# Retention and SSD layer on eight cores: state outputs in tile layout, keys scaled at evacuation, less work on GpSimd, new scheduling constants

## The chip, the cores and the metric

The kernel runs on one Trainium2 chip (trn2), the same program on all 8 cores, each with its own requests. The metric is the device time of the slowest core, in microseconds (us). Every run also gives the span of each core and its mean granted TensorE clock. Some executions of these kernels were in a second, slower state, in which some cores show a lower clock and the time is longer: cores 4 and 5 at 0.933 to 0.939, where the same kernel's fast runs had every core at 0.964 or more. Such runs are marked slow here, and comparisons use fast runs alone.

Names in the profile: PE is TensorE, PEld its weight load, DVE is VectorE, ACT ScalarE, POOL GpSimd, SP the sync engine that issues many of the transfers.

## The reference, cut

One layer of a hybrid backbone, shortened here (casts and some arguments are left out). Two groups of tokens share the weights: context (two sequences of 256 per core) and latent (one sequence of 1024 per core, scans starting from given states).

```python
def trunk_layer(x, mod, rope, s_ret0, s_ssd0, p):
    sh1, sc1, g1, sh2, sc2, g2 = jnp.split(mod, 6, axis=-1)
    h = x * (1 + sc1) + sh1
    proj = h @ p['w_in']
    q, k, v, g, z, xbc, dt_raw = jnp.split(proj, IN_SPLITS, axis=-1)
    ...                                   # retention: 4 heads, chunked two-way scan, gated RMS norm
    o_ret, sr_f, sr_b = bidir_scan(q, k, v, v, lg_f, lg_b, s_ret0[0], s_ret0[1])
    ...                                   # Mamba-2 SSD: 8 heads, conv, chunked two-way scan
    y, ss_f, ss_b = bidir_scan(cm, bm, xsf * dt_f[..., None], xsf * dt_b[..., None], la_f, la_b, ...)
    o_ssd = (rms_norm(y * silu(z)) * p['ssd_norm_w']).astype(x.dtype)
    mix = jnp.concatenate([o_ret, o_ssd], axis=-1) @ p['w_out']
    x = layer_norm(ALPHA * x + g1 * mix, p['ln1_g'], p['ln1_b'])
    h2 = x * (1 + sc2) + sh2
    ffn = (silu(h2 @ p['w_gate']) * (h2 @ p['w_up'])) @ p['w_down']
    x = layer_norm(ALPHA * x + g2 * ffn, p['ln2_g'], p['ln2_b'])
    return x, s_ret, s_ssd                # the context's final states are outputs too
```

Inside a scan the state of a chunk is the sum over its tokens of tail · kᵀv: the decay `tail` may be put on the keys or on the values.

## The kernel before

The kernel is a Python program that builds a graph of operations. A list scheduler then gives each operation an engine and a place in that engine's order, by a cost model of its own, and an allocator lays all buffers into one arena. So an edit to one operation can move everything else. Times that the scheduler believes are called *planned* below; they are not times of the chip. The parts that the argument touches:

```python
# constants of the scheduler: priorities, order of stages, ring depths, and LD: after which buffer's
# work a weight load is let go
LV = dict(ht=1.1, conv=0.5, ..., retA=1.3, retB=1, ..., evB=0.5, outA=1.6, outB=0.9, ...)
SEQ = ("ssdA", "headA", "ssdB", "ada", "headB", "outA", "outB")
LD = dict(..., wo0="a0", wo1="a3", ..., ln1="oB", g0="b2", g1="b0", ...)
# ... cut ...
    oret_d = do("oret", [2, 2, 4, 128, 128])          # context states, retention
    ossd_d = do("ossd", [2, 2, 8, 128, 64])           # context states, SSD
# ... cut ...
    def affine(out, in_, scale, bias, eng=(ACT, DVE)):
        ...
        if DVE in eng:
            alts[DVE] = (vcost(DVE, out, [in_], "ts") + 0.08,
                         lambda e: e.tensor_scalar(out=R(out), in0=R(in_), scalar1=R(scale), scalar2=R(bias), op0=ALU.mult, op1=ALU.add))
# ... cut ...  a weight slab loaded as f32 in halves, and cast on the core
    def half_load(name, dst, src, q, after=()):
        s = P.buf("%s_f%d" % (name, q), 2048)
        o = P.dma(SP, s, src[:, q * 2048:(q + 1) * 2048], after=after)
        for i in range(2):
            cp(dst[:, q * 2048 + i * 1024:q * 2048 + (i + 1) * 1024], s[:, i * 1024:(i + 1) * 1024], (ACT, DVE, POOL))
# ... cut ...  start: small biases of the convolution, and the scaled input hs1 (xT1 is the second latent half)
            affine(hs3[ck][:, kt, :], xT[(ck, q)][...], sc1p[q][:, kt % 4, c:c + 1], 0.0)
        ts(nb3[:, f, :], p3, -1.0, ALU.mult)
        tt(cb3[:, f, :], p3, wsum[:, f].unsqueeze(2).to_broadcast([128, 4, 2]), ALU.mult)
# ... cut ...  SSD block: small row copies feed a matmul's operand, on the SP queue
        for s_ in range(3):
            P.dma(SP, sx[96 + s_:97 + s_, :].rearrange("p (r n) -> p r n", r=16), rsT[g][32 * s_:32 * s_ + 16, tok])
# ... cut ...  retention head: values scaled by tail from SBUF or PSUM, keys transposed and copied
                tt(vs[...], vsrc[...], tailw4[:, d, h, :]..., ALU.mult, EN["vs"])
            cp(kt_[:, c_ * 512:c_ * 512 + 512], ps, (ACT, DVE))
            P.dma(SP, oret_d[:, :, h].rearrange("s d p e -> p s d e"), stS.rearrange("p (s d e) -> p s d e", s=2, d=2), is_out=True)
# ... cut ...  the parameters of the first layer norm, multiplied in on GpSimd, one token tile at a time
    late.append((P.dma(SP, ln1, brow(R_LN1G, 2048)), "ln1"))
            tt(x1[t], x1[t], ln1[:, 0:1024], ALU.mult, POOL)
            tt(x1[t], x1[t], ln1[:, 1024:2048], ALU.add, POOL)
```

Of the kernel before, what the change touches and what calls it, by code (L numbers as in the profile page):

```python
# [22 lines left out]
class Op:  # L23
    __slots__ = ("idx", "eng", "alts", "is_dma", "nbytes", "deps", "inc", "cval", "fin", "npend", "succ", "start", "key",
                 "allocs", "touch", "sem", "is_out", "table", "tag", "cost", "ready", "done", "fn", "w", "pal")

    def __init__(self, idx, alts, key, tag):
        self.idx, self.alts, self.key, self.tag = idx, alts, key, tag
        self.eng, self.fn, self.cost = None, None, 0.0
        self.is_dma, self.nbytes, self.deps, self.inc, self.cval = False, 0, set(), False, 0  # L30
        self.fin = self.start = 0.0
        self.npend, self.succ, self.allocs, self.touch = 0, [], [], []
        self.sem, self.is_out, self.table, self.ready, self.done = None, False, None, 0.0, False
        self.w, self.pal = [], []
# [90 lines left out]
class Prog:  # L125
# [17 lines left out]
    def add(self, alts, reads, writes, table=None, after=()):  # L143
# [33 lines left out]
        for a in after:  # L177
            if a is not None:
                o.deps.add(a)
        return o  # L180
# [30 lines left out]
    def schedule(self, extra):  # L211
# [85 lines left out]
        busy = {e: 0.0 for e in ENGS}  # L297
        while nd < n:
# [41 lines left out]
            st = max(t, o.ready)  # L340
            if o.allocs:
# [19 lines left out]
            o.eng, o.fn, o.cost, o.start, o.done = e, fn, cost, st, True  # L361
            tcur[e] = st + cost
# [27 lines left out]
    def place(self, slack):  # L390
        live = []
        for b in self.bufs:
            if not b.ops:
                b.off = 0
                continue
            t0 = min(min([o.start] + [a.start for a in o.pal]) for o in b.ops)
            t1 = max(o.fin for o in b.ops)
            live.append((t0, t1, b))
# [41 lines left out]
    def emit(self, stack):  # L440
# [61 lines left out]
        def make(engname):  # L502
# [32 lines left out]
LV = dict(ht=1.1, conv=0.5, tm=1.1, prep=1, ssdA=1, ssdB=1.1, ssdi=0, retA=1.3, retB=1, reti=0.02, headA=2, headB=1.7, evA=0, evB=0.5, outA=1.6,  # L535
          outB=0.9, evoA=0.7, evoB=0.7, ada=1.2)
OPT = dict(rope="")
ENG = dict(yn="V", vs="VP", wg="VP", y2="P", g="")
SEQ = ("ssdA", "headA", "ssdB", "ada", "headB", "outA", "outB")
RING = dict(W=3, P=2, y1=2, y2=2, yb=2, xw=3, Sd=3, Sf=3, Sfb=1, hB=3, hA=4, vs=1, kt=2, PT=1, sq=2, rg=1, qf=3, rp=2, xr=3)  # L540
LD = dict(w2="x1", h10="p1A", h11="p0B", a4="p0B", a5="p1A", h12="z11", a6="p1B", a8="z3", h13="z3", a7="b0", a9="a3", wo0="a0", wo1="a3", h00="a2",
          h01="a2", a10="a2", a11="b1", h02="oA", h03="b1", rope="z7", S0f="oA", xr1="b1", xr0="b1", gate01="a2", gate00="b3", ln1="oB", g0="b2", g1="b0",
          g2="oB", g3="b2", g4="oB", g5="f0", g6="f4", g7="f4", g8="f5", g9="f2", g10="f3", wd0="f4", wd1="f5", wd2="f9", wd3="f10", ln2="f10", gate11="f9",
# [5 lines left out]
C_CVEC, C_BADA, C_CONVW, C_CONVB, C_LN1G, C_LN1B, C_N = 0, 16, 64, 104, 112, 120, 128  # L549
# [33 lines left out]
def build():  # L583
# [19 lines left out]
    oret_d = do("oret", [2, 2, 4, 128, 128])  # L603
    ossd_d = do("ossd", [2, 2, 8, 128, 64])
# [49 lines left out]
    def vcost(eng, out, ins, kind):  # L654
# [5 lines left out]
        if any(inps(v) for v in ins):  # L660
            return 0.17 + n * 0.00103
        if kind in ("copy", "ts"):
            return 0.12 + n * 0.00075
# [34 lines left out]
    def affine(out, in_, scale, bias, eng=(ACT, DVE)):  # L698
# [3 lines left out]
        if DVE in eng:  # L702
# [48 lines left out]
    def half_load(name, dst, src, q, after=()):  # L751
# [3 lines left out]
        for i in range(2):  # L755
            cp(dst[:, q * 2048 + i * 1024:q * 2048 + (i + 1) * 1024], s[:, i * 1024:(i + 1) * 1024], (ACT, DVE, POOL))
# [42 lines left out]
    nwb = P.buf("nwb", 512)  # L799
    P.dma(SP, nwb, brow(R_NW, 512), after=[xl[7]])  # L800
# [85 lines left out]
    for ct in range(8):  # L886
        for j in range(5):
            ts(diagw4[:, ct, j, :], ident_f, cols[:, C_CONVW + ct * 5 + j:C_CONVW + ct * 5 + j + 1], ALU.mult, eng=(DVE, POOL))
    dI = P.buf("dI", 1024, BF16)
    dI3 = dI.rearrange("p (h m) -> p h m", h=8)  # L890
    for h in range(8):
        ts(dI3[:, h, :], ident_f, smalls[:, 32 + h:33 + h], ALU.mult, eng=(DVE, POOL))
# [282 lines left out]
    nws = P.buf("nws", 512)  # L1175
# [10 lines left out]
    def state_update(d, t, S, nxt):  # L1186
# [4 lines left out]
        tt(v8(xw), v8(xs_tm[t]), bc8(w), ALU.mult, POOL)  # L1191
# [7 lines left out]
        tt(v8(sd), v8(S), bc8(EXPO[g][:, q, 32 + d * 8:40 + d * 8]), ALU.mult, POOL)  # L1199
# [5 lines left out]
    def ssd_seq(g, t0, nb, s0):  # L1205
# [8 lines left out]
        for i in range(nb - 1, -1, -1):  # L1214
            if S is not None:
                Rb[i] = P.buf("R%d" % (t0 + i), 512, BF16)
                cp(Rb[i], S, (ACT, POOL))
# [4 lines left out]
        if not s0:  # L1222
            P.dma(SP, ossd_d[(t0 - 8) // 2, 1].rearrange("h n e -> n h e"), v8(S), is_out=True)
# [4 lines left out]
        for i in range(nb):  # L1228
# [3 lines left out]
            if S is not None:  # L1232
                Sb = rSfb()
                cp(Sb, S, (ACT, POOL))
# [6 lines left out]
        if not s0:  # L1241
            P.dma(SP, ossd_d[(t0 - 8) // 2, 0].rearrange("h n e -> n h e"), v8(S), is_out=True)
# [3 lines left out]
    def ssd_block(g, t, Sb, Rb):  # L1246
# [43 lines left out]
        tt(y1, cur, z_tm[t], ALU.mult, DVE if cur is y else POOL)  # L1290
# [4 lines left out]
        yn, yb = ry2(), ryb()  # L1295
        tt(yn, y1, nws, ALU.mult, EN["yn"])
        affine(yb, yn, sm[:, 1:2], 0.0, (ACT,))
# [4 lines left out]
        cp(oT[t // 4][:, :, o_:o_ + 128], ps.rearrange("p (j t) -> p j t", j=4), (ACT, DVE))  # L1302

    P.level = LV_BG
    ts(nws, nwb, math.sqrt(512.0), ALU.mult)
# [7 lines left out]
    rvs = {GA: Ring("vsA", RING["vs"], 1024, BF16), GB: Ring("vsB", RING["vs"], 1536, BF16)}  # L1313
    rkt = {GA: Ring("ktA", RING["kt"], 512, BF16), GB: Ring("ktB", RING["kt"], 1024, BF16)}
# [6 lines left out]
    def ret_unit(h, ck, b0, T, v3, cross):  # L1321
# [6 lines left out]
        for d in range(2):  # L1328
            if cross[0]:
                qf[d] = rqf()  # L1330
                tt(c2(qf[d]), c2(q), b2(rowt4[:, h, d, :]), ALU.mult, (DVE, POOL))
# [19 lines left out]
        tt(rg, rg, T["g"][:, b0:b0 + 512], ALU.mult, POOL)  # L1351
# [5 lines left out]
    def head(g, h, wload, lv):  # L1357
# [5 lines left out]
        for j, name in ((0, "q"), (1, "k"), (3, "g")):  # L1363
            for c_, ck in enumerate(CK[g]):
# [7 lines left out]
                else:  # L1372
# [10 lines left out]
                    tt(b, tA, tB, ALU.add, POOL)  # L1383
        vs = rvs[g]()
        voff = lambda d, j: (d * 4 + j) * 128
        for c_, ck in enumerate(CK[g]):
# [7 lines left out]
            for d in range(2):  # L1394
                a_, n_ = (0, 4) if g == GA or c_ == d else ((2, 2) if c_ == 0 else (0, 2))
                v0 = voff(d, c_ * 4 + a_)
                vsrc = T["v"][:, c_ * 512:c_ * 512 + 512] if "P" in ENG["vs"] else ps
                tt(vs[:, v0:v0 + n_ * 128].rearrange("p (c j e) -> p c j e", j=2, e=128), vsrc[:, a_ * 128:(a_ + n_) * 128].rearrange("p (c j e) -> p c j e", j=2, e=128),
                   tailw4[:, d, h, :].unsqueeze(1).unsqueeze(3).to_broadcast([128, n_ // 2, 2, 128]), ALU.mult, EN["vs"])
# [3 lines left out]
        kt_ = rkt[g]()  # L1403
        for c_ in range(len(CK[g])):
# [3 lines left out]
            cp(kt_[:, c_ * 512:c_ * 512 + 512], ps, (ACT, DVE))  # L1408
        k3 = kt_.rearrange("p (j e) -> p j e", e=128)
        v3 = T["v"].rearrange("p (j e) -> p j e", e=128)  # L1410
        vt = lambda d, j: vs[:, voff(d, j):voff(d, j) + 128]
        if g == GA:
            ps = P.ps("mix")
            for s_ in range(2):
                for d in range(2):
                    for j in range(2):
                        mm(ps[:, (s_ * 2 + d) * 128:(s_ * 2 + d) * 128 + 128], k3[:, s_ * 2 + j, :], vt(d, s_ * 2 + j), j == 0, j == 1)
            stS = rstS()
            cp(stS, ps, (ACT, DVE))
            P.dma(SP, oret_d[:, :, h].rearrange("s d p e -> p s d e"), stS.rearrange("p (s d e) -> p s d e", s=2, d=2), is_out=True)  # L1420
            ret_unit(h, 2, 0, T, v3, [[], []])
        else:
            pu = [P.ps("mix"), P.ps("mix", 256)]
            for s_ in range(3):
                for d in range(2):
                    c = 3 - s_ if d else s_
                    for j in range(2):
                        mm(pu[s_ // 2][:, (s_ % 2) * 256 + d * 128:(s_ % 2) * 256 + d * 128 + 128], k3[:, c * 2 + j, :], vt(d, c * 2 + j), j == 0, j == 1)
# [4 lines left out]
            for s_ in range(3):  # L1433
                t_, sb = rSt(), rSb()
                tt(de(t_), prev, gd, ALU.mult, (DVE, POOL))
                u = pu[s_ // 2][:, (s_ % 2) * 256:(s_ % 2) * 256 + 256]
                if s_ < 2:
                    sf = rSr()
                    tt(sf, t_, u, ALU.add)
                    cp(sb, sf, (ACT, POOL))  # L1440
# [159 lines left out]
    def stage(name):  # L1600
# [19 lines left out]
        elif name == "headB":  # L1620
# [3 lines left out]
            cp(S0b, S0f, (POOL,))  # L1624
# [37 lines left out]
def _prep_inputs(inp):  # L1662
# [39 lines left out]
    for i in range(8):  # L1702
# [7 lines left out]
        cols[:, C_LN1B:C_LN1B + 8] = f(inp["ln1_b"])[0].reshape(8, 128).T  # L1710
        m = dict(shared)
# [21 lines left out]
```

## Time and profile before

| | before |
|---|---|
| time, median of 4 runs | 766.73 us (763.62 to 767.23) |
| spans of the 8 cores in the profiled run | 742.1 to 762.4, mean 753.7 us |
| core 5 (slowest): PE / DVE / ACT / POOL busy | 88 / 55 / 39 / 44% |

First the table of busy time by stretch of time, for core 5. Each column of an engine is its busy time in that stretch, with the count of instructions; then come the granted clock, the share of the DMA engines and their rate. TensorE's idle time in a stretch is the stretch less its busy time.

```profile
core 5: us, PE busy (x) PEld busy (x) DVE busy (x) ACT busy (x) POOL busy (x), PEclk, DMA share, GB/s
0.00:80.00 80.00, 50.75 (x471) 28.44 (x471) 36.74 (x118) 37.11 (x69) 27.03 (x76) 0.91 0.92 228
80.00:200.00 120.00, 111.56 (x879) 63.03 (x880) 91.69 (x183) 91.00 (x145) 76.18 (x88) 0.97 0.53 102
200.00:240.00 40.00, 20.82 (x169) 12.48 (x166) 19.84 (x32) 18.10 (x31) 17.79 (x21) 0.74 0.85 155
240.00:360.00 120.00, 105.81 (x912) 63.47 (x913) 107.30 (x175) 61.76 (x101) 82.15 (x84) 1.00 0.49 106
...
400.00:430.00 30.00, 19.76 (x109) 12.27 (x108) 22.91 (x24) 12.87 (x19) 16.22 (x9) 0.83 0.47 106
430.00:740.00 310.00, 310.00 (x1438) 140.52 (x1437) 100.32 (x177) 56.05 (x92) 100.61 (x71) 1.00 0.28 61
```

Read it from the bottom. From 430 us on TensorE is busy all the time, so what happens there can only shift. All that can be won lies in the idle time before: 29.2 us at the start, 19.2 us in 200 to 240, 14.2 us in 240 to 360, 10.2 us in 400 to 430. Two of these are single waits. The timeline of core 5 near 216 us (start, duration, engine, operation; in brackets the idle time before it and what ended it):

```profile
215.96 0.22 PE L622 MATMUL psum<-arena 128*128 128x128 bf16 x1 [2.02 <-DVE arena L670]
232.06 2.18 PE L622 MATMUL psum<-arena 128*128 128x256 bf16 x8 [15.88 <-DVE arena L670]
...
208.81 4.50 POOL L670 TENSOR_TENSOR arena<-arena 128x512 bf16<-128x512 bf16 x4 [2.69 <-ACT arena L647]
227.54 0.59 POOL L185 DMA_DIRECT2D arena<-w_out  x1 [14.23 <-DMA oret<-arena]
```

TensorE's wait is put down to DVE, but DVE had nothing to do either: GpSimd held its queue for 14.23 us, because the load of w_out that stood next in it takes over the buffer of a retention state whose output (oret) had not landed. The view of one tensor (oret) says how long such outputs took, on the same core:

```profile
who waited for it (us, times):
  POOL arena L185: 14.2, 1
...
DMA to landing us min/median/max: 2.5/9.8/25.4
```

Over the eight cores the worst landing is 21.8 to 29.5 us. Cores 0, 1, 4, 5 and 7 wait 10.6 to 14.2 us so, the other three do not.

The second wait, again the timeline of core 5:

```profile
406.22 15.59 POOL L670 TENSOR_TENSOR arena<-arena 128x4 f32<-128x4 f32 x7 [5.59 <-DVE arena L670]
...
407.36 2.24 DVE L684 SCALAR_TENSOR_TENSOR arena<-arena 128x4 f32<-128x4 f32 x1 [1.29 <-POOL arena L670]
409.70 12.39 DVE L704 TENSOR_SCALAR arena<-arena 128x512 f32<-128x512 f32 x5
...
420.08 1.08 PE L625 MATMUL psum<-arena 128*128 128x128 f32 x4 [10.17 <-DVE arena L704]
420.96 2.34 PE L622 MATMUL psum<-arena 128*128 128x512 bf16 x5
```

Five of DVE's affines (scale and bias of a tile, `affine` above) take 2.48 us each (12.39 over 5), just while GpSimd runs its layer-norm multiplies (the merged line of 15.59 us). Even an operation on four elements takes 2.24 us there. (Where lines are merged, one shape is printed for all: most of the 7 on GpSimd are 1024 wide.)

### The profile page before, as it was taken

Reading aid. Unit: us, or ns where it says so; the run is one execution under the profiler, and the core shown is the slowest. Engines: PE = TensorE matmul, PEld = TensorE weight load, DVE = VectorE, ACT = ScalarE, POOL = GpSimd, SP = SyncE. Lnnn points to the kernel's source line nnn. Section 1 sums busy time; section 2 is a strip of 40 time slices with the busy share of each in tenths; the row PEclk is TensorE's granted clock in tenths of the full one; section 3 lists DMA queues with packets and bytes.
Section 4 is the critical chain, followed back from the end, with each engine's and each line's share of the span. In section 5 each row is a group of like instructions: output and inputs, shape, how many; then the busy total and the mean of one; then the engine's idle time right before and its main releaser. Section 6 shows DMA issues by size and latency. Waiting matters only on the chain.

```text
span 762.4 us, 13147 instructions; the slowest of 8 cores (742.1 to 762.4 us)
## 1 busy us (share of the span) xinstructions
PE 668.6 (88%) x4212; PEld 343.9 (45%) x4212; DVE 420.1 (55%) x796; ACT 301.0 (39%) x490; POOL 338.8 (44%) x363
## 2 busy tenths in 40 slices
PE   0599899998827998788995999999999999999993
PEld 0246554555514554546442544444444444444441
DVE  5525567868837968998588421212121212256775
ACT  2646697875734533576544221111111110021122
POOL 5313154797627757586107198300000000039975
PEclk9889999999967999999998899999999999999997
DMA  8989746276386019943037030319700055002122
GB/s 243 325 131 220 155 82 123 46 128 146 59 166 125 2 34 204 217 102 84 28 115 162 1 56 6 70 37 179 139 1 1 1 103 139 21 0 111 57 83 83
DMA packets 20306, 75.93 MB, mean 100 GB/s; under 512 B 7072, under 2 KB 9376, under 8 KB 13584
## 3 DMA queue, kind: packets, MB, share of 16 engines
q0 software_dynamic: 5440, 40.77, 30.2%
q1 hardware_dynamic: 14800, 34.33, 14.3%
q8 instruction: 36, 0.59, 0.3%
q14 instruction: 30, 0.25, 0.1%
HBM read 107.29 MB, written 8.40 MB: 152 GB/s over the span
## 4 chain that ended last, share of the span: by engine, by line
PE 68%; DMA 14%; DVE 8%; issue 5%; POOL 3%; SPq 1%; ACT 1%; DVEq 0%; POOLq 0%; ACTq 0%
PE psum L622 67%; DMA arena<-w_in 5%; DVE arena L670 5%; DMA oret<-arena 3%; DMA arena<-xT 3%; POOL arena L670 2%; DMA arena<-w_ada 2%; DVE arena L704 1%; PE psum L625 1%; SPq L185 1%; DVE arena L684 1%; ACT arena L647 1%; DVE arena L695 1%; POOL arena L185 0%; DVE psum L1263 0%
## 5 line engine op out<-in xcount | busy, mean ns | idle before, releaser
L622 PE MATMUL psum<-arena 128*128 128x512 bf16 (+7 forms) x4104 | 658.0, 318 | 70.0 <-ACT arena L647 29.3
L622 PEld LDWEIGHTS psum<-arena 128*128 128x128 bf16 (+2 forms) x4104 | 331.2, 99 | 391.0 <-issue 108.2
L670 POOL TENSOR_TENSOR arena<-arena 128x512 f32<-128x512 f32 (+7 forms) x219 | 278.6, 1293 | 137.4 <-DVE arena L670 85.1
L647 ACT ACTIVATE arena<-psum 128x512 bf16<-128x512 f32 (+3 forms) x199 | 107.3, 552 | 247.1 <-PE psum L622 239.4
L647 ACT ACTIVATE arena<-arena 128x512 bf16<-128x512 f32 (+8 forms) x155 | 106.5, 716 | 178.6 <-DVE arena L684 117.4
L670 DVE TENSOR_TENSOR arena<-arena,psum 128x512 bf16<-128x512 bf16 (+4 forms) x110 | 71.0, 646 | 170.9 <-PE psum L622 161.1
L670 DVE TENSOR_TENSOR arena<-psum,arena 128x512 f32<-128x512 f32 (+4 forms) x166 | 106.6, 654 | 77.8 <-PE psum L622 54.3
L670 DVE TENSOR_TENSOR arena<-arena 128x512 bf16<-128x512 bf16 (+10 forms) x132 | 81.0, 621 | 12.3 <-ACT arena L647 3.2
L647 ACT ACT_TABLE_LOAD x42 | 53.9, 1283 | 17.9 <-PE psum L622 12.9
L684 DVE SCALAR_TENSOR_TENSOR arena<-arena 128x512 f32<-128x512 f32 (+2 forms) x60 | 45.8, 768 | 9.6 <-POOL arena L670 5.8
L185 POOL DMA_DIRECT2D arena<-w_down x4 | 2.1, 529 | 102.1 <-PE psum L622 102.0
L704 DVE TENSOR_SCALAR arena<-arena 128x512 bf16<-128x512 f32 (+1 forms) x51 | 38.8, 806 | 9.5 <-DMA arena<-xT 9.1
L695 POOL CAST arena<-arena 128x2 bf16<-128x2 f32 (+3 forms) x66 | 22.5, 377 | 42.2 <-ACT arena L647 10.3
L647 ACT ACTIVATE arena<-psum,arena 128x512 bf16<-128x512 f32 (+2 forms) x58 | 35.6, 649 | 12.6 <-PE psum L625 6.3
L185 POOL DMA_DIRECT2D arena<-w_gu x11 | 6.4, 579 | 72.4 <-PE psum L622 65.9
L695 DVE CAST arena<-psum 128x512 bf16<-128x512 f32 (+2 forms) x47 | 29.5, 645 | 12.8 <-PE psum L622 8.9
L625 PE MATMUL psum<-arena 128*128 128x128 f32 (+1 forms) x108 | 15.7, 284 | 11.5 <-DVE arena L704 10.2
L676 POOL TENSOR_SCALAR arena<-arena 128x128 bf16<-128x128 f32 (+1 forms) x30 | 15.8, 539 | 11.4 <-DMA arena<-rows 5.2
L625 PEld LDWEIGHTS psum<-arena 128*128 128x128 f32 (+1 forms) x108 | 13.1, 146 | 14.8 <-issue 13.3
L1263 DVE COPY_PREDICATED psum<-arena,psum 128x512 f32<-128x512 uint16 x24 | 16.6, 691 | 4.2 <-PE psum L622 4.1
L695 DVE CAST arena<-arena 128x1024 bf16<-128x1024 f32 (+7 forms) x24 | 9.8, 420 | 10.6 <-DMA arena<-w_ada 4.4
L676 DVE TENSOR_SCALAR arena<-arena 128x128 bf16<-128x128 f32 (+7 forms) x61 | 13.8, 270 | 2.1 <-ACT arena L647 0.5
(19 smaller groups left out, 51.5 us busy)
## 6 DMA issues: line engine op xcount, KB each, us to landing
arena<-w_gu POOLq DMA_DIRECT2D x11, 1024.0 KB, 10.0
arena<-w_in POOLq DMA_DIRECT2D x10, 1024.0 KB, 14.6
arena<-w_ada POOLq DMA_DIRECT2D x10, 1024.0 KB, 16.2
arena<-xT SPq DMA_DIRECT2D x6, 1024.0 KB, 20.3
arena<-x SPq DMA_DIRECT2D x12, 512.0 KB, 4.5
arena<-w_down POOLq DMA_DIRECT2D x4, 1408.0 KB, 15.1
y<-arena SPq DMA_DIRECT2D x11, 512.0 KB, 2.7
arena<-w_ada SPq DMA_DIRECT2D x4, 1024.0 KB, 15.6
```

The source lines that it names most:

```text
L185: o = self.add({eng: (0.9 if eng == POOL else 0.45, lambda e: e.dma_start(out=R(out), in_=R(in_)))}, [in_], [out], after=after)
L622: return P.add({PE: (c, lambda e: e.matmul(R(out), lhsT=R(lhsT), rhs=R(rhs), start=start, stop=stop))}, [lhsT, rhs], [out])
L625: return P.add({PE: (0.12, lambda e: e.transpose(out=R(out), in_=R(in_), identity=R(ident_f)))}, [in_, ident_f], [out])
L647: fn = lambda e: e.activation(out=R(out), in_=R(in_), func=func, **{k: R(v) for k, v in kw.items()})
L670: fn = lambda e: e.tensor_tensor(out=R(out), in0=R(in0), in1=R(in1), op=op)
L676: fn = lambda e: e.tensor_scalar(out=R(out), in0=R(in0), scalar1=R(s1), scalar2=None, op0=op0)
L684: fn = lambda e: e.scalar_tensor_tensor(out=R(out), in0=R(in0), scalar=R(scalar), in1=R(in1), op0=op0, op1=op1, **{k: R(v) for k, v in kw. ...
L695: alts[g] = (vcost(g, out, [in_], "copy"), lambda e: e.tensor_copy(out=R(out), in_=R(in_)))
L704: lambda e: e.tensor_scalar(out=R(out), in0=R(in_), scalar1=R(scale), scalar2=R(bias), op0=ALU.mult, op1=ALU.add))
L1263: P.add({DVE: (0.7, lambda e, eb=eb, ef=ef, mk_=mk_: e.copy_predicated(R(eb), R(mk_), R(ef)))}, [mk_, ef, eb], [eb])
```

## The change

Its intent: states leave as the tiles lie, in one run of 2 KB per partition, in place of runs of 512 B (oret) and 256 B (ossd), and the host puts them in order; DVE scales the keys while it takes them out of PSUM, so that no scaled copy of the values and no plain copy of the keys is needed; the weight of the SSD norm is multiplied in where the transposed tile leaves PSUM; casts and copies are taken off GpSimd; the diagonal matrices that the convolution and the SSD skip term multiply by (identity times a weight; GpSimd built 18 of the 48 before) are all built on DVE; the scheduler's model adds time to a DVE operation that it marks (`lock`) when it would start during a marked GpSimd operation; and the constants were tuned anew. The core of the diff:

```diff
@@ scheduler @@
+            if o.lock and e == DVE and lockint[0] <= st < lockint[1]:
+                cost += 0.7 * (lockint[1] - st)
@@ allocator: slack is 0 in both builds, so this does nothing @@
-            t1 = max(o.fin for o in b.ops)
+            t1 = max(o.fin + (3.0 * slack if o.is_out else 0.0) for o in b.ops)
@@ constants (LV, RING and the rest of LD cut) @@
-ENG = dict(yn="V", vs="VP", wg="VP", y2="P", g="")
-SEQ = ("ssdA", "headA", "ssdB", "ada", "headB", "outA", "outB")
+ENG = dict(dg="V", wg="V", y2="P", xw="P", sd="P", zm="P", qf="VP", rg="P", ra="P", rd="VP")
+SEQ = ("ssdA", "headA", "ssdB", "ada", "outA", "headB", "outB")
-LD = dict(..., wo1="a3", ..., ln1="oB", ...)
+LD = dict(..., wo1="a1", ..., ln1="f0", ...)
@@ outputs @@
-    oret_d = do("oret", [2, 2, 4, 128, 128])
-    ossd_d = do("ossd", [2, 2, 8, 128, 64])
+    oret_d = do("oret", [4, 128, 512])
+    ossd_d = do("ossd", [2, 2, 128, 512])
-            P.dma(SP, oret_d[:, :, h].rearrange("s d p e -> p s d e"), stS.rearrange("p (s d e) -> p s d e", s=2, d=2), is_out=True)
+            P.dma(SP, oret_d[h], stS, is_out=True)
@@ affine, SBUF to SBUF of one type @@
+            alts[DVE] = (vcost(DVE, out, [in_], "tt"),
+                         lambda e: e.scalar_tensor_tensor(out=R(out), in0=R(in_), scalar=R(scale), in1=R(bias).to_broadcast([128, n_]), op0=ALU.mult, op1=ALU.add))
@@ casts of half slabs; other copies likewise from POOL to DVE @@
-            cp(dst[...], s[...], (ACT, DVE, POOL))
+            cp(dst[...], s[...], (ACT, DVE))
@@ SSD norm weight @@
-        tt(yn, y1, nws, ALU.mult, EN["yn"])
-        affine(yb, yn, sm[:, 1:2], 0.0, (ACT,))
+        affine(yb, y1, sm[:, 1:2], 0.0, (ACT,))
-        cp(oT[t // 4][:, :, o_:o_ + 128], ps.rearrange("p (j t) -> p j t", j=4), (ACT, DVE))
+        tt(oT[t // 4][:, :, o_:o_ + 128], ps.rearrange("p (j t) -> p j t", j=4), nwc.unsqueeze(2).to_broadcast([128, 4, 128]), ALU.mult)
@@ retention keys @@
-                tt(vs[...], vsrc[...], tailw4[:, d, h, :]..., ALU.mult, EN["vs"])
-            cp(kt_[:, c_ * 512:c_ * 512 + 512], ps, (ACT, DVE))
+                tt(cj(ks[:, k0:k0 + n_ * 128]), cj(ps[:, a_ * 128:(a_ + n_) * 128]), tailw4[:, d, h, :]..., ALU.mult)
```

## The prediction

Sum: -10, -7, -5 and +2 come to -20 us. "Locked" and "locks" stand for what was measured before: DVE operations that took longer beside GpSimd's, the affine 2.4 us at the layer norm against 0.54 us in the tail, and in 240 to 360 us on core 5 the scalar_tensor_tensor of 128x512 0.68 to 1.30 us (mean 1.00) in the six cases that overlap a GpSimd tensor_tensor, 0.68 us in the two that do not. The output of 2.5 us "on a quiet queue" is the one issued at 184.17 us, with a DMA share of 0.39 in 184 to 186.5 us; in 214 to 228 us, in the stall, the share was 0.90.

> **What bounds the kernel now.** The profiled run took 763.4 us. From 430 us on TensorE is saturated: the stretch 430 to 740 is 310.0 us busy at clock 1.00 on core 5, 215 ns per 512-wide matmul. The change touches nothing there. TensorE's waits on the slowest core (view of waits) are: 14.5 us at the start, behind DMA (share 0.92 in the first 80 us), not touched; 15.9 us near 216 us for DVE; 10.2 us near 410 us for DVE's layer-norm affine; and some 12 us of small waits between 240 and 400 us, where DVE is busy 107 of 120 us.
>
> 1. *216 us.* All engines stop for 14 to 16 us. The timeline shows GpSimd holding its queue 14.2 us for a w_out load that waits for a retention-state output to land (25.4 us at worst, 2.5 us on a quiet queue): the load takes over that output's buffer. Those outputs leave as 512-byte runs among three weight loads. Cores 0, 1, 4, 5 and 7 wait 10.6 to 14.2 us so; cores 2, 3 and 6 do not and end at 742, 752 and 749 us. So the metric, the slowest core, gains less than the wait.
> 2. *410 us.* Four DVE tensor_scalar take 9.9 us, 2.4 each, against 0.54 alone in the tail. GpSimd runs 1024-wide LN1 multiplies (2.37 us each) just then. [...]
>
> **What changes.** State outputs become one 2 KB run per partition. In the changed order w_out waits for no late output. Two other loads do wait for outputs, the fourth context head's (ossd) and the first latent head's (oret); I expect waits under 4 us. The new buffer-lifetime padding is multiplied by a slack that is 0 in both builds, so it does nothing. The LN1 parameter load moves behind the first FFN slab, so GpSimd has no multiplies at the second layer norm; DVE's affine (now a scalar_tensor_tensor, about 0.7 us) is split evenly with ScalarE.
>
> GpSimd instructions fall from 321 to 270, DVE's rise from 748 to 769, ScalarE's fall from 412 to 394; matmuls stay 4208. In the latent heads DVE loses eight value scalings, three key copies, and some decays (about 14 us) and gains 16 key scalings from PSUM at 0.68 and 0.41 us and three copies (about 10). In the SSD blocks the same kind of exchange gives about -3 us. GpSimd loses about 5 and 12 us there, so fewer locked DVE instructions.
>
> **Sum (estimates):** -10 us for the output wait as the slowest core sees it, -7 for the layer norm, -5 for the DVE-bound stage and locks, +2 for new load waits: about 745 us. Range 731 to 757. Faster by over 2%: 0.68; within 2%: 0.28; slower: 0.04.
>
> **What would show it.** No GpSimd DMA issue waiting over 5 us for oret or ossd; oret landing under 10 us even amid loads; the wait before the second layer norm's transposes at 3 to 4 us; DVE busy in the latent heads a few us lower; spans of cores nearer each other; last 310 us unchanged.
>
> **What would make it wrong.** A new queue block by ossd or oret at other loads (worth 10 us); added early DVE work (18 more diagonal builds at 0.3 us) delaying the first evictions; rescheduling making DVE or ScalarE late in the SSD and head stages; scalar_tensor_tensor still blocked by GpSimd.

## The result

The changed kernel is correct. Its first four runs were 744.65, 745.49, 758.59 and 760.84 us, the last two slow (cores 4 and 5 at a clock near 0.935). The ratio of its fast runs to those of before is 0.9726, with a 95% interval of 0.9681 to 0.9771. A ratio here is the mean time of one kernel's fast runs over that of the other's of the same rounds, so it is not quite the ratio of the medians quoted. The medians quoted, those of the kernel before too, count slow runs where there were any. Measured again on another chip it gave 744.97 us (742.67 to 745.98, four fast runs) against 765.35, ratio 0.9725 [0.9700, 0.9751]. So the change is worth 21 us, and the predicted 745 us was met. The spans of the cores are 729.0 to 744.4 us, mean 737.8 (before: 753.7).

The same views of the changed kernel, on its slowest core, 3. First the stretches:

```profile
0.00:80.00 80.00, 39.58 (x384) 20.26 (x384) 36.22 (x135) 35.88 (x64) 6.79 (x26) 0.87 0.94 229
80.00:200.00 120.00, 116.42 (x911) 66.88 (x912) 87.92 (x180) 93.71 (x149) 64.97 (x104) 0.99 0.55 105
200.00:240.00 40.00, 33.31 (x295) 18.05 (x294) 29.85 (x48) 23.25 (x36) 20.00 (x23) 0.87 0.84 150
240.00:360.00 120.00, 109.28 (x894) 67.09 (x893) 98.98 (x177) 64.14 (x95) 63.08 (x66) 0.97 0.46 102
...
400.00:430.00 30.00, 29.96 (x155) 15.36 (x154) 11.48 (x17) 12.22 (x18) 7.51 (x4) 1.00 0.27 69
430.00:740.00 310.00, 299.39 (x1388) 135.53 (x1385) 108.57 (x195) 55.88 (x91) 121.44 (x85) 0.99 0.27 65
```

In 430 to 740 us, where TensorE is busy for 283.9 to 299.4 of the 310 us, the granted clock is 0.98 to 0.99 on all eight cores. The stall at 200 to 240 us and the wait at 400 to 430 us are gone, the two stages between are tighter, and **the start is worse**: 40.4 us idle against 29.2.

The wait near 216 us has become a wait of 3.28 us for a weight load and one of 0.95 us for row copies (timeline):

```profile
222.15 1.86 PE L634 MATMUL psum<-arena 128*128 128x512 bf16 x4 [3.28 <-DMA arena<-w_in]
224.97 10.72 PE L634 MATMUL psum<-arena 99*128 99x512 bf16 x54 [0.95 <-DMA arena<-arena]
```

No GpSimd instruction waits for an output of oret, and for one of ossd only on cores 0, 4 and 7, 0.9 to 1.1 us. Yet the outputs of oret still land late, in the view of that tensor:

```profile
DMA to landing us min/median/max: 5.1/11.1/19.2
```

At the second layer norm (timeline) the small operation takes 0.16 us in place of 2.24, five affines take 0.69 us each (2.08 over 3, 1.41 over 2), and TensorE goes over to its transposes (L637) without a wait:

```profile
399.31 0.16 DVE L698 SCALAR_TENSOR_TENSOR arena<-arena 128x4 f32<-128x4 f32 x1 [1.29 <-POOL arena L684]
399.59 2.08 DVE L719 SCALAR_TENSOR_TENSOR arena<-arena 128x512 f32<-128x512 f32 x3
...
402.23 1.41 DVE L719 SCALAR_TENSOR_TENSOR arena<-arena 128x512 f32<-128x512 f32 x2
...
404.13 1.47 PE L637 MATMUL psum<-arena 128*128 128x128 f32 x12
```

And the start. Before, on core 5:

```profile
67.03 12.13 PE L622 MATMUL psum<-arena 128*128 128x2 bf16 x119 [1.17 <-DVE arena L670]
82.13 8.08 PE L622 MATMUL psum<-arena 128*128 128x256 bf16 x67 [2.97 <-ACT arena L647]
```

After, on core 3:

```profile
71.30 0.99 PE L634 MATMUL psum<-arena 128*128 128x2 bf16 x32 [5.69 <-DVE arena L684]
80.12 10.23 PE L634 MATMUL psum<-arena 128*128 128x512 bf16 x74 [7.83 <-DVE arena L684]
...
69.28 1.28 DVE L722 TENSOR_SCALAR arena<-arena 128x512 bf16<-128x512 f32 x3 [4.54 <-DMA arena<-xT]
78.55 0.88 DVE L722 TENSOR_SCALAR arena<-arena 128x512 bf16<-128x512 f32 x2 [6.93 <-DMA arena<-xT]
```

Two waits of 5.69 and 7.83 us are new. DVE was itself waiting for the second latent half of the input (xT), which lands near 69 and 78 us; the small bias operations that TensorE needs stood behind those affines in DVE's order, and TensorE's own order had the projection of that same half next.

To compare kernels without picking a core, the next table gives TensorE's idle time by stretch as the mean of all eight cores, each worked out as stretch less busy time as above, from the one profiled execution of each kernel. Stretches are fixed in time, so a kernel that is later at one place shifts work into the next.

| kernel, mean idle us | 0–80 | 80–200 | 200–240 | 240–360 | 360–430 | sum |
|---|---|---|---|---|---|---|
| before | 28.1 | 7.5 | 14.4 | 13.5 | 10.3 | 73.9 |
| after | 38.2 | 4.0 | 4.7 | 11.0 | 1.9 | 59.8 |

So the 14 us of idle time that were won are 24 us won and 10 us lost. The sum of the idle time falls 14.1 us and the mean span falls 15.9.

### The profile page after: what moved, and what is told of

It is laid out like the page before. It is cut to its first block, busy times and chain, and to the rows that moved or that the text cites. A ratio compares the mean times of both kernels' runs of the same rounds, so it can differ in the third digit from the quotient of the medians.

```text
span 744.4 us, 13000 instructions; the slowest of 8 cores (729.0 to 744.4 us)
## 1 busy us (share of the span) xinstructions
PE 666.2 (89%) x4212; PEld 342.3 (46%) x4212; DVE 404.5 (54%) x817; ACT 302.2 (41%) x478; POOL 291.4 (39%) x312
## 4 chain that ended last, share of the span: by engine, by line
PE 64%; DMA 12%; issue 8%; DVE 7%; POOL 4%; ACT 1%; SPq 1%; DVEq 0%; POOLq 0%; ACTq 0%
PE psum L634 64%; DMA arena<-xT 7%; DVE arena L684 4%; POOL arena L684 4%; DMA arena<-w_ada 4%; DVE arena L698 1%; SPq L191 1%; ACT arena L659 1%; DMA arena<-arena 1%; PE psum L637 1%; DVE arena L719 1%; DVE arena L722 1%; DVE arena L709 0%; DVEq L518 0%; POOL arena L191 0%
## 5 line engine op out<-in xcount | busy, mean ns | idle before, releaser
L634 PE MATMUL psum<-arena 128*128 128x512 bf16 (+6 forms) x4104 | 655.2, 318 | 63.0 <-ACT arena L659 29.5
L634 PEld LDWEIGHTS psum<-arena 128*128 128x128 bf16 (+1 forms) x4104 | 330.8, 99 | 384.0 <-issue 100.5
L684 POOL TENSOR_TENSOR arena<-arena 128x512 f32<-128x512 f32 (+6 forms) x204 | 257.4, 1282 | 185.1 <-DVE arena L684 116.3
L659 ACT ACTIVATE arena<-psum 128x512 bf16<-128x512 f32 (+2 forms) x180 | 99.8, 571 | 222.5 <-PE psum L634 204.3
L684 DVE TENSOR_TENSOR arena<-arena,psum 128x512 bf16<-128x512 bf16 (+3 forms) x134 | 86.6, 653 | 181.0 <-PE psum L634 175.8
L684 DVE TENSOR_TENSOR arena<-psum,arena 128x512 bf16<-128x512 f32 (+5 forms) x202 | 127.8, 650 | 57.4 <-PE psum L634 48.1
L684 DVE TENSOR_TENSOR arena<-arena 128x1 f32<-128x1 f32 (+10 forms) x87 | 38.6, 444 | 10.2 <-PE psum L634 3.2
L709 DVE CAST arena<-psum 128x512 bf16<-128x512 f32 (+2 forms) x29 | 17.7, 622 | 17.7 <-PE psum L634 15.4
L709 DVE CAST arena<-arena 128x512 bf16<-128x512 f32 (+8 forms) x39 | 21.5, 557 | 10.7 <-DMA arena<-w_ada 4.3
L719 DVE SCALAR_TENSOR_TENSOR arena<-arena 128x512 f32<-128x512 f32 x25 | 19.6, 828 | 0.7
L690 DVE TENSOR_SCALAR arena<-arena 128x128 bf16<-128x128 f32 (+6 forms) x79 | 16.6, 260 | 5.0 <-ACT arena L659 4.1
L722 DVE TENSOR_SCALAR arena<-arena 128x512 bf16<-128x512 f32 x27 | 12.8, 510 | 11.6 <-DMA arena<-xT 11.5
L637 PE MATMUL psum<-arena 128*128 128x128 f32 (+1 forms) x108 | 14.4, 275 | 0.2 <-DVE arena L684 0.2
## 6 DMA issues: line engine op xcount, KB each, us to landing
arena<-w_in POOLq DMA_DIRECT2D x10, 1024.0 KB, 11.8
arena<-w_down POOLq DMA_DIRECT2D x4, 1408.0 KB, 15.9
arena<-w_ada SPq DMA_DIRECT2D x4, 1024.0 KB, 15.3
```

What stands on the lines that cost most here:

```text
L634: return P.add({PE: (c, lambda e: e.matmul(R(out), lhsT=R(lhsT), rhs=R(rhs), start=start, stop=stop))}, [lhsT, rhs], [out])
L637: return P.add({PE: (0.12, lambda e: e.transpose(out=R(out), in_=R(in_), identity=R(ident_f)))}, [in_, ident_f], [out])
L659: fn = lambda e: e.activation(out=R(out), in_=R(in_), func=func, **{k: R(v) for k, v in kw.items()})
L684: fn = lambda e: e.tensor_tensor(out=R(out), in0=R(in0), in1=R(in1), op=op)
L690: fn = lambda e: e.tensor_scalar(out=R(out), in0=R(in0), scalar1=R(s1), scalar2=None, op0=op0)
L709: alts[g] = (vcost(g, out, [in_], "copy"), lambda e: e.tensor_copy(out=R(out), in_=R(in_)))
```

## The experiments

Eleven edited kernels were run, and the changed kernel once more as a yardstick. All gave correct results. Runs of one group shared a chip and the runs of the kernel before.

### Parts of the change, put into the kernel before (before on this chip: 766.17 us)

**Layout of the outputs alone.** The order of every engine is the same as before.

```diff
-    oret_d = do("oret", [2, 2, 4, 128, 128])
-    ossd_d = do("ossd", [2, 2, 8, 128, 64])
+    oret_d = do("oret", [4, 128, 512])
+    ossd_d = do("ossd", [2, 2, 128, 512])
-            P.dma(SP, oret_d[:, :, h].rearrange("s d p e -> p s d e"), stS.rearrange(...), is_out=True)
+            P.dma(SP, oret_d[h], stS, is_out=True)      # ossd and the host's reordering likewise
```

> The kernel before with one edit: the four retention-state and four SSD-state outputs leave as one 2 KB run per partition. The order on every engine is unchanged. Theory A (the prediction's: the 512-byte and 256-byte runs made the output slow): the retention output among the weight loads lands in under 10 us instead of 25, GpSimd's wait for it before the second w_out load (10.6 to 14.2 us on five cores) falls under 2 us, and the fast runs come to about 757 us, ratio 0.985 to 0.99. Rival B (the output stands behind megabytes of weight loads whatever its runs; what took the wait away in the changed kernel is that no load takes over a late output's buffer): it still lands in 15 to 25 us, the wait stays over 8 us on most cores, ratio 0.995 to 1.0. In the changed kernel's trace these outputs still take 15 to 21 us at worst, which speaks for B.

Measured: 757.96 us (755.91 to 767.89, one run slow), ratio 0.9888 [0.9866, 0.9910], so 8.6 us. The worst landing of oret falls from 21.8–29.5 to 12.0–16.0 us on the eight cores, and GpSimd's wait for it is gone except on core 1 (4.8 us). TensorE's wait at the second layer norm stays at 10.1 us. On core 5 the view of oret now says:

```profile
DMA to landing us min/median/max: 2.4/9.4/12.5
```

The layout removes the stall, as the prediction said; landing under 10 us did not come true. GpSimd's wait was for oret; what the runs of ossd add was not tried alone.

**LN1 parameters loaded late, alone.**

```diff
-LD = dict(..., ln1="oB", ...)
+LD = dict(..., ln1="f0", ...)
```

> The kernel before with one edit: the LN1 parameter load waits for the first FFN slab instead of the latent output projection, as in the changed kernel. Only GpSimd's order differs: its LN1 multiplies come after the second layer norm. Theory [...]: the four tensor_scalar of the second layer norm take about 0.55 us each instead of 2.4, TensorE's wait before the transposes falls from 10.2 to 2 to 4 us on every core, ratio about 0.99 (7 us). Rival (the wait is ScalarE's or the statistics chain's, and DVE only ends last by chance): the wait stays over 7 us, ratio over 0.996.

Measured: 753.78 us (752.82 to 755.42), ratio 0.9843 [0.9821, 0.9865], so 12.0 us. The mean idle time in 360 to 430 us falls from 10.3 to 0.4 us. On core 4 the timeline shows why: the same tensor_scalar now takes 0.47 us (2.37 over 5), the small operation 0.16 us.

```profile
409.79 0.16 DVE L684 SCALAR_TENSOR_TENSOR arena<-arena 128x4 f32<-128x4 f32 x1 [1.29 <-POOL arena L670]
410.06 2.37 DVE L704 TENSOR_SCALAR arena<-arena 128x512 f32<-128x512 f32 x5
```

The gain is larger than the wait of 10.2 us. One reason is in the lines of before above: after its stall TensorE is slow, 1.08 us for four fp32 transposes, where four took 0.60 us before the stall (at 401.74 us), and 2.34 us for five 512-wide matmuls, against some 215 ns for one such matmul later (310.0 us over 1438), so 1.3 us on these five alone (2.34 less 5 × 0.215). The granted clock of that core was 0.50 from 420 to 424 us, 0.86 from 424 to 426 and 1.00 from 426 to 428, and 1.00 from 396 to 409 us before the stall; with the late load it is 1.00 in 400 to 430 us. How much of the rest comes from the clock was not worked out.

**The new form of the affine alone**, at the old planned cost, so that no order changes.

```diff
-            alts[DVE] = (..., lambda e: e.tensor_scalar(..., scalar1=R(scale), scalar2=R(bias), ...))
+            alts[DVE] = (..., lambda e: e.scalar_tensor_tensor(..., scalar=R(scale), in1=R(bias).to_broadcast([128, n_]), ...))
```

> The kernel before with one edit: DVE's affine from SBUF to SBUF in one type is a scalar_tensor_tensor with the bias broadcast, at the old planned cost, so that no engine's order changes. GpSimd's LN1 multiplies stay beside it. If the form of the instruction was what freed DVE: about 0.7 us each, TensorE's wait falls from 10.2 to under 5 us, ratio 0.992 to 0.995. If an instruction with two SBUF inputs is held by GpSimd just as well: about 2.4 us each, the wait stays at 9 to 11 us, ratio 1.0. I expect the second.

Measured: 767.98 us (760.07 to 770.5), ratio 1.0022 [1.0000, 1.0044]. The new form, whose second input is one column broadcast along the row, is held no less, 2.77 us each (11.07 over 4) on core 5, where it took 0.69 us in the changed kernel with no GpSimd multiplies beside it, and TensorE's wait for it is 11.2 us on all eight cores:

```profile
397.42 11.07 DVE L705 SCALAR_TENSOR_TENSOR arena<-arena 128x512 f32<-128x512 f32 x4
```

So the layer norm was not saved by the form of the instruction.

**The new constants alone** (LV, SEQ, RING, LD, which include the late LN1 load).

```diff
-SEQ = ("ssdA", "headA", "ssdB", "ada", "headB", "outA", "outB")     # and LV, RING, LD
+SEQ = ("ssdA", "headA", "ssdB", "ada", "outA", "headB", "outB")     # as in the changed kernel
```

> The kernel before with the changed kernel's tuning constants alone: stage order, priorities, ring sizes and the places from which loads may start. Operations, engines' alternatives and output layout stay. If the gain is the schedule's: ratio 0.965 to 0.98, no second-layer-norm wait, and the start as in the kernel before, with no new TensorE wait between 60 and 80 us. If the gain needs the lighter DVE and GpSimd work or the output layout: ratio 0.98 to 1.0, with DVE busy about as before between 240 and 360 us (107 of 120 us) and, since a load for the adaLN weights here waits for the second retention output, a new GpSimd wait for it.

Measured: 759.39 us (756.45 to 789.79, one run slow), ratio 0.9903 [0.9880, 0.9925], so 7.4 us where the late LN1 load alone gives 12.0. The wait at the layer norm is gone and the start is as before (28.8 us idle). The wait of GpSimd for the second retention output that was expected came on no core; with the old layout another wait comes, of 8.8 to 12.5 us on seven of the eight cores. On core 2 (timeline):

```profile
232.76 7.92 PE L622 MATMUL psum<-arena 99*128 99x512 bf16 x45 [11.01 <-DMA arena<-arena]
```

TensorE waits for the small row copies of an SSD block, which go through the same SP queue as the outputs.

### The changed kernel taken apart, and the two main edits together (before on this chip: 765.35 us)

**The yardstick**, not edited.

> The changed kernel, not edited, as the yardstick on this chip. Fast runs 744 to 750 us, ratio to before 0.970 to 0.977. Again TensorE waits of 5 to 8 us for DVE near 71 and 80 us, each behind a DVE affine of the second latent half that itself waits for its input load.

Measured: 744.97 us, ratio 0.9725, as given above. On cores 3 and 5 the two waits at the start are 4.4 to 5.1 and 8.3 to 9.1 us (the profile puts the second down to ScalarE, which had its own affines of that half to do).

**Old layout in the changed kernel**, orders unchanged (the diff of the layout in reverse).

```diff
-            P.dma(SP, oret_d[h], stS, is_out=True)
+            P.dma(SP, oret_d[:, :, h].rearrange("s d p e -> p s d e"), stS.rearrange(...), is_out=True)   # ossd likewise
```

> The changed kernel with the old layout of the two state outputs (512-byte and 256-byte runs), orders of all engines unchanged. Theory A (the layout is worth several us in the changed order too, since later loads take over the output's buffers and small loads queue behind it): outputs of the retention state land at worst at 22 to 30 us, a wait of 5 us or more for them or behind them comes back on some core between 200 and 240 us, and the time rises 4 to 12 us. Theory B (the new order alone had already moved every load away from a late output): landing as late, but no wait over 3 us, and the time within 3 us of the changed kernel.

Measured: 754.50 us (753.93 to 755.04), ratio 0.9854 [0.9832, 0.9876], so 9.5 us worse than the changed kernel by the medians. On cores 0, 3, 5 and 6 TensorE waits 10.8 to 11.9 us for row copies, and oret lands at worst 24.2 to 28.4 us after its issue there. The other four cores have no such wait and land at 19.3 to 20.4 us. Theory A holds, by another route than the prediction's: no load waits for the output's buffer, but the row copies do not come through. The timeline of core 0:

```profile
233.82 6.47 PE L634 MATMUL psum<-arena 99*128 99x512 bf16 x34 [10.78 <-DMA arena<-arena]
...
218.02 0.53 SPq L191 DMA_DIRECT2D oret<-arena  x1
233.58 0.52 SPq L191 DMA_DIRECT2D arena<-arena  x1
```

The same place in the yardstick, core 5:

```profile
218.05 0.53 SPq L191 DMA_DIRECT2D oret<-arena  x1
220.30 0.51 SPq L191 DMA_DIRECT2D arena<-arena  x1
```

With 512-byte runs the SP engine issues the next row copy 15.6 us after the output, since it waits for the one before to land (the view of SP's waits has 15.0 us for it); with 2 KB runs, 2.3 us after. Why a 4 KB copy takes so long there was not measured by itself.

**Two edits in the kernel before: layout and late LN1.** Nothing else.

```diff
-            P.dma(SP, oret_d[:, :, h].rearrange("s d p e -> p s d e"), stS.rearrange(...), is_out=True)
+            P.dma(SP, oret_d[h], stS, is_out=True)      # ossd likewise
-LD = dict(..., ln1="oB", ...)
+LD = dict(..., ln1="f0", ...)
```

> The kernel before with two edits only: the new output layout and the LN1 parameter load moved behind the first FFN slab. Theory A (the two waits are separate and add up): ratio 0.971 to 0.975, as fast as the whole change, so the rest of the change (key scaling, casts, transposed norm weight, new constants) is worth nothing net. Theory B (they overlap, or the first merely shows another wait): ratio 0.980 to 0.985, the better of the two alone, and the rest of the change is worth some 6 to 8 us.

Measured: 742.98 us (742.13 to 745.18, five fast runs), ratio 0.9712 [0.9687, 0.9737]. The two gains add up (0.9888 × 0.9843 = 0.9733), and these few lines are as fast as the whole change (0.9725). All the rest of the change is worth nothing net that these runs can show.

**A later planned arrival.** The scheduler of the changed kernel is told that the second latent half lands 9 us later than it thinks. No operation is added or taken away; the order changes, and some operations change engine with it (on core 3 DVE has 831 instructions in place of 817, ScalarE 461 in place of 478).

```diff
                 o.fin = srv[0] + 1.2
+                if o.tag == "start" and any(b.name.startswith("xT1_") for b in o.bufs_):
+                    o.fin += 9.0
```

> The changed kernel, where the kernel's own scheduler is told that the second half of the latent input lands 9 us later than it thinks (it thinks 58 to 61 us, the trace shows 69 to 79). No operation differs; the order does, on all engines; the small bias operations of DVE come ahead of the affines that wait for that half. Theory A (the start loss of the changed kernel is the engine order, a plan that believes in an early load): the two waits of TensorE near 71 and 80 us go, TensorE's idle time in 0 to 80 us falls from about 40 to about 30 us, and the time falls 6 to 10 us, to 735 to 740 us. Theory B (the start loss is the added work of the early DVE, the diagonal builds): TensorE's idle time in 0 to 80 us stays at 37 to 42 us, and the time within 2 us of the changed kernel. Later stages are reshuffled too; a loss there is read by stage.

Measured: 739.50 us (739.04 to 741.54, four fast runs), ratio 0.9663 [0.9639, 0.9687]. The start is as theory A says; on core 3 the stretches and, below, the timeline:

```profile
0.00:80.00 80.00, 50.14 (x480) 28.87 (x481) 39.08 (x143) 41.04 (x74) 9.81 (x57) 0.89 0.94 228
...
240.00:360.00 120.00, 104.65 (x859) 63.79 (x857) 95.31 (x166) 58.13 (x89) 59.94 (x62) 0.97 0.46 102
```

```profile
68.01 22.29 PE L637 MATMUL psum<-arena 128*128 128x2 bf16 x211 [1.01 <-DVE arena L687]
```

TensorE now works through 68 to 90 us without a wait, in 211 matmuls, while DVE still waits for the late half until 78.89 us. Its idle time there is back at 30 us. The time falls only 5.5 us of the 6 to 10 expected (4.7 between the means of the fast runs), because the order of everything later moved too: on this core 15.4 us idle in 240 to 360 us, where the changed kernel had 10.7.

### The start and the layer norm once more (before on this chip: 765.28 us)

**GpSimd may cast half slabs again** in the changed kernel; the diagonal builds stay on DVE.

```diff
-            cp(dst[...], s[...], (ACT, DVE))
+            cp(dst[...], s[...], (ACT, DVE, POOL))
```

> The changed kernel, where GpSimd may again take the casts of the half-size weight slabs, as in the kernel before; nothing else is edited. That alone makes the scheduler put the first slab's load later and the second latent half's planned arrival back to where the kernel before had it, so DVE's small bias operations stand ahead of the affines again. Theory A (taking those casts off GpSimd is what caused the start loss, through the plan): TensorE's idle time in 0 to 80 us falls from 40 to 28 to 33 us, no wait of over 3 us for DVE between 62 and 82 us; the time falls 3 to 8 us against the changed kernel (its ratio 0.972), to 0.962 to 0.968, unless a later stage gives it back. Theory B (the loss came from the diagonal builds and copies that moved to DVE and ScalarE): idle time 37 us or more, time within 2 us of the changed kernel.

Measured: five of seven runs were slow; the two fast ones are 739.23 and 741.56 us, ratio 0.9689 with a wide interval [0.9620, 0.9758]. The profile is of a slow run too, where cores 0, 1, 6 and 7 had the low clock (0.81 in 80 to 200 us, where the other four had 0.99 to 1.00); on those other four the mean idle time in 0 to 80 us is 29.5 us, in 240 to 360 us 15.4 us. On core 3:

```profile
0.00:80.00 80.00, 49.67 (x471) 28.03 (x471) 39.27 (x136) 37.43 (x70) 17.36 (x60) 0.91 0.91 228
```

Two cores of each die were disturbed, so this profile is weaker evidence than one of a fast run; but in 0 to 80 us no core of the eight has over 30.3 us. So the start loss goes when the casts may use GpSimd, although all diagonal builds are still DVE's. The time agrees with theory A, but two fast runs settle no figure for it.

**LN1 parameters early again**, in the changed kernel; the orders of TensorE, DVE and ScalarE stay the same.

```diff
-LD = dict(..., ln1="f0", ...)
+LD = dict(..., ln1="oB", ...)
```

> The changed kernel with the LN1 parameter load back at its old, early place, so that GpSimd runs its 1024-wide LN1 multiplies at the second layer norm again; the orders of TensorE, DVE and ScalarE stay the same. Theory A (GpSimd running next to DVE is what held the layer norm; who shares the affine and in which form doesn't matter): DVE's affines there take 2 us or more each instead of 0.75, a wait of TensorE of 4 to 9 us appears near 400 us, and the time rises 4 to 9 us, to 0.977 to 0.985. Theory B (in the changed order the even split with ScalarE or the new form has already taken the wait away): no wait over 2 us there, time within 2 us of the changed kernel.

Measured: fast runs 758.01 to 759.31 us, ratio 0.9927 [0.9881, 0.9974], some 15 us worse than the changed kernel (0.9927 less 0.9725, of 765 us; from the two intervals, good to about 4 us). That is more than expected, and so is TensorE's wait, 11.1 to 11.2 us on all eight cores. Core 0 (timeline):

```profile
414.64 2.79 PE L637 MATMUL psum<-arena 128*128 128x128 f32 x12 [11.09 <-DVE arena L719]
...
398.32 2.24 DVE L698 SCALAR_TENSOR_TENSOR arena<-arena 128x4 f32<-128x4 f32 x1 [1.29 <-POOL arena L684]
400.67 8.22 DVE L719 SCALAR_TENSOR_TENSOR arena<-arena 128x512 f32<-128x512 f32 x3
408.82 0.68 DVE L684 TENSOR_TENSOR arena<-arena,psum 128x512 bf16<-128x512 bf16 x1
409.42 4.97 DVE L719 SCALAR_TENSOR_TENSOR arena<-arena 128x512 f32<-128x512 f32 x2
...
397.18 28.66 POOL L684 TENSOR_TENSOR arena<-arena 128x4 f32<-128x4 f32 x12 [5.38 <-DVE arena L684]
```

These lines show best how DVE slows next to GpSimd. GpSimd is busy without a gap from 397 to 426 us. From 398 to 414 us all of DVE's operations with every input in SBUF take 2.2 to 2.7 us, the one on four elements too. The one at 408.82, with one input in PSUM, takes 0.68, as the same operation does after GpSimd's run (0.69 at 428.91 us).

**New constants and new layout, old operations**, in the kernel before.

```diff
-            P.dma(SP, oret_d[:, :, h].rearrange("s d p e -> p s d e"), stS.rearrange(...), is_out=True)
+            P.dma(SP, oret_d[h], stS, is_out=True)      # ossd likewise
-SEQ = ("ssdA", "headA", "ssdB", "ada", "headB", "outA", "outB")     # and LV, RING, LD
+SEQ = ("ssdA", "headA", "ssdB", "ada", "outA", "headB", "outB")     # as in the changed kernel
```

> The kernel before with the new scheduling constants (which include the late LN1 load) and the new output layout, but none of the changed operations. Theory A (constants, LN1 place and layout are the whole gain, and the changed operations gain at the DVE-bound stage only what they lose at the start): the 11.7 us wait behind the small row copies, seen with the constants alone, goes; ratio 0.968 to 0.976, TensorE idle in 0 to 80 us 28 to 31 us, in 240 to 360 us 13 us or more. Theory B (the changed operations carry gain of their own): ratio 0.978 or more.

Measured: fast runs 749.0 to 751.22 us (three slow ones more), ratio 0.9810 [0.9755, 0.9864]. The wait behind the row copies is gone, and the start is as before (28.8 us), as theory A said; but the ratio is what theory B said. Compared with the changed kernel, which adds the new operations and the scheduler's lock model and engine choices, mean idle time is 5.0 us more in 80 to 200, 3.0 in 200 to 240, 5.8 in 240 to 360 us, and 9.3 less at the start. So these together do carry a gain of their own with these constants, and most of it is lost again at the start. The intervals of the two ratios nearly touch ([0.9700, 0.9751] for the yardstick, on another chip), so the size of the net gain is uncertain.

### A last attempt (before on this chip: 765.52 us)

The planned arrival 6 us later in place of 9.

```diff
-                    o.fin += 9.0
+                    o.fin += 6.0
```

> The changed kernel with the scheduler told that the second half of the latent input lands 6 us later than it thinks, not 9. Looked for: a version that keeps the start of the 9 us build (TensorE idle 30 us in 0 to 80 us, against 40 in the changed kernel) without its dearer latent heads (TensorE idle 15 us in 240 to 360 us, against 10.6). If the gain is the start alone: ratio 0.960 to 0.966, 735 to 740 us, idle time in 0 to 80 us 28 to 32 us. If 6 us is too little for the plan to change at the start: idle 37 us or more there, and 743 us or more.

Measured: 743.16 us (740.0 to 747.28, six fast runs), ratio 0.9710 [0.9690, 0.9730]. The mean idle time is 30.6 us at the start and 12.4 in 240 to 360 us, both between those of the two builds; but in the profile, which is of the slowest of the six runs, the slowest core, at 746.1 us, has 65.2 us of idle time in all where the mean is 55.9, and 8.5 us of it in 80 to 200 us. By the times it is no better than the 9 us build, which stays the best found.

The mean idle times side by side (for the casts on GpSimd, the four cores without the low clock):

| kernel | ratio | 0–80 | 80–200 | 200–240 | 240–360 | 360–430 | sum |
|---|---|---|---|---|---|---|---|
| before + layout | 0.9888 | 29.5 | 6.9 | 9.0 | 13.2 | 10.2 | 68.8 |
| before + late LN1 | 0.9843 | 28.7 | 8.4 | 13.9 | 13.6 | 0.4 | 65.0 |
| before + new affine form | 1.0022 | 28.4 | 7.5 | 9.1 | 13.1 | 11.8 | 70.0 |
| before + constants | 0.9903 | 28.8 | 8.4 | 15.3 | 17.0 | 0.4 | 70.0 |
| before + layout + late LN1 | 0.9712 | 28.5 | 7.5 | 8.6 | 12.9 | 0.3 | 57.8 |
| before + constants + layout | 0.9810 | 28.8 | 9.0 | 7.7 | 16.8 | 0.1 | 62.4 |
| after, once more (yardstick) | 0.9725 | 38.5 | 3.8 | 4.4 | 10.9 | 2.1 | 59.6 |
| after, old layout | 0.9854 | 38.0 | 3.8 | 8.6 | 11.5 | 2.1 | 64.0 |
| after, LN1 early | 0.9927 | 38.7 | 3.9 | 4.5 | 10.8 | 13.2 | 71.1 |
| after, casts on GpSimd | 0.9689 | 29.5 | 4.1 | 7.2 | 15.4 | 2.2 | 58.3 |
| after, arrival 9 us later | 0.9663 | 28.8 | 4.4 | 5.0 | 14.5 | 2.1 | 55.0 |
| after, arrival 6 us later | 0.9710 | 30.6 | 5.1 | 5.4 | 12.4 | 2.4 | 55.9 |

Each row is one execution. That of the new affine form is the one without the stall, so its 9.1 us in 200 to 240 us say nothing of the affine.

## Why the prediction was right, and where it was wrong

The time came out as predicted, 745 us. Not all terms of the sum did; the wrong ones erred in opposite directions, so that the total came out exact was luck.

1. **"-10 us for the output wait as the slowest core sees it": right.** The layout alone gave 8.6 us in the old order, and taking it back cost 9.5 us in the new one. Two details were wrong. The outputs were to land "under 10 us even amid loads"; the worst took 12 to 16 us with the layout alone and 15.9 to 21.2 us in the yardstick. And the prediction saw only the load that takes over the output's buffer. In the new order the short runs hurt in another way, by holding up the row copies.
2. **"-7 for the layer norm": right in cause, too small.** It is 12.0 us alone, and some 15 when undone in the changed kernel. The prediction left a wait of "3 to 4 us" there; TensorE's mean idle time in 400 to 430 us fell from 8.5 to 0.2 us with this edit alone, to 0.1 us in the changed kernel, and the granted clock in that stretch is 1.00 (core 3) where it was 0.83 (core 5 before). It named two reasons, no GpSimd multiplies and a new split of the affine; only the first counts. Its worry that the new form is "still blocked by GpSimd" is shown to be true (2.77 us each in the affine experiment), and did no harm since in the changed kernel no GpSimd multiply runs beside it (0.69 us each).
3. **"-5 for the DVE-bound stage and locks": about right.** Mean idle time fell 3.5 us in 80 to 200 and 2.5 us in 240 to 360 us, and DVE's busy time in the latter from 107.3 to 99.0 us (core 5 before, core 3 after). With new constants and old operations the idle time there was 16.8 us, so it is the operations, with the lock model and the engine choices, that bring this, not the constants.
4. **"+2 for new load waits": right in size, not in cause.** The term stood for loads that wait for outputs, and those waited 1.1 us at most, for ossd. What TensorE waits for is the landing of w_in near 222 us, 3.3 us on the slowest core; cores 3 and 6 of the kernel before, which have no stall, have the same wait there (3.4 and 3.3 us).
5. **The start, "14.5 us at the start, behind DMA, … not touched": the step that failed.** The sum has no term for it, and mean idle time there rose by 10 us. The prediction named a danger, the 18 more diagonal builds on DVE. That was the wrong culprit: with those builds still on DVE, both a later planned arrival and the casts given back to GpSimd bring the idle time to 29 us. What changed is the order. In the scheduler's plan (read from the program, not from the chip) the first weight slab's load goes out 1.3 us earlier once no GpSimd cast precedes it; then the second latent half is planned ahead of a weight load that it stood behind before, and believed to be in at 58 to 61 us rather than 67 to 70. In the traces DVE gets its two parts at 71.4 and 80.3 us before (core 5) and at 69.3 and 78.6 us in the changed kernel (core 3): the plan moved by some 8 us, the data by 2. The engines then stand in order behind data that is not there.

Why did an error of 10 us not show in the total? With the sizes that held in the changed kernel's own order the sum is roughly 9.5 for the layout, 15 for the layer norm, 6 for the stages between and 10 lost at the start, so 20.5 us, where 21 were measured: the layer norm was so much better than its term that it covered the start. (The first two are differences of times, the second good to about 4 us only, the others mean idle times, so this is a rough sum, and that it closes within 0.5 us means little.) What stays open is how much the new operations are worth with a good start. The 9 us build is 4.7 us faster than the changed kernel by the means of fast runs, but it loses 3.5 us of mean idle time in 240 to 360 us to its reshuffled order, and no run has the good start with the old middle.

## What to carry to other kernels

Add up a change by stage and test its parts alone: here two edits of a few lines, contiguous outputs and one load moved later, equal the whole rewrite within the noise, and a total that met the prediction hid a loss of 10 us. Read the same stage on all cores and in more than one execution: the stall near 216 us came on five cores of eight in one profile and on none at full length in another of the same order. When a scheduler sets the order, removing an operation from an engine can move its plan; compare planned arrivals with those in the trace and look for engines that stand before data still in flight. DVE's affines took 2.48 us each next to GpSimd's multiplies and 0.47 us without; moving the GpSimd work won 12.0 us, while the other form of the DVE instruction that was tried gained nothing (ratio 1.0022).
